# The opening group's two quads take x together: four output banks per k-tile, and the opening loads in one fixed line

## The chip, the cores and the metric

The kernel runs on one core of one Trainium2 chip. The metric is the device time in microseconds (us) of one execution. Three runs of the kernel before took 868.64, 869.21 and 869.86 us (median 869.21). A separate profiled execution gave the trace that is read here.

The engines go by short names: PE is TensorE (matmuls), PEld its weight loads, DVE is VectorE, ACT is ScalarE, POOL is GpSimd, SP is SyncE, which issues nearly all DMA transfers. A name such as SPq or ACTq means the sequencer that issues DMAs.

## The reference

One layer of a hybrid decoder: meta tokens are put ahead of the sequence, the input is normalised, projected by one matrix into eight parts, and goes through a gated short convolution and a chunkwise retention; an output projection, the residual and a last norm follow. What the change touches is the first part of the projection.

```python
h = jnp.concatenate([meta_b, x], axis=1)        # 16 meta rows, then 2048 rows of 1024
hn = rms_norm(h, norm_g)
proj = jnp.einsum('bld,de->ble', hn, w_in)      # w_in: 1024 x 4096
cx, cb, cc, cg, q, k, v, rg = jnp.split(proj, N_PROJ, axis=-1)
conv_out = short_conv_branch(cx, cb, cc, conv_w) * jax.nn.silu(cg)
...
mixed = jnp.concatenate([conv_out, ret_out], axis=-1)
return h + jnp.einsum('ble,ed->bld', mixed, w_out)
```

All of it is in float32. The kernel gets that precision by splitting each operand into a high part and a low part (`mh`, `ml` for x and for the opening's weights, `wh`, `wl` for later weights) and adding three products.

## The kernel before, in words

**Tiles.** The sequence is worked in two blocks of 1024 rows (`r` = 0, 1), each in two column halves `j` of 512. The contraction over 1024 is cut into eight k-tiles of 128, four to a half. A *quad* is one pair of projection parts (2 x 128 output columns) for a block, so four output tiles 128x512, each in one PSUM bank. The pool `pj` has four banks, the pool `ms` four others for everything small.

**Two kinds of quad.** `quad` (L236) forms a quad by seven products of sums of blocks (Strassen's scheme); it needs sums and differences of x-blocks, held in `m[2]`, `m[3]`, `m[4]`, `m[6]`, and of weight blocks. `stationary` makes the weight blocks: POOL forms sums and differences in place (L121, L124, L124, L151), ACT casts the high parts (L112), DVE subtracts to get the low parts (L113). `quad_plain` (L293) forms a quad the ordinary way, 96 matmuls, and needs no sums. The first group of all, a convolution group (`group_plain`), uses it twice, since x is still arriving then: the first quad is `first[0]` (parts CC and CX), the second `first[1]` (CG and CB). Head 0 with its first `quad` comes next.

**The opening.** The x-tiles (256 KB each, eight per column half) are loaded by SP in `load_x`, scaled and split: ACT makes `mh` (L115), DVE `ml` (L116). The weights of the first quad are loaded in two pieces for the two blocks that are needed first (128 columns on ACT's queue, 384 on SP's), the other two whole (`begin`). `moving` runs over j, half and k-tile, and calls hooks after given tiles. `normalise_meta` prepares the meta rows, `meta_products` (L456) multiplies the raw weight blocks with them, and `block_sums` (L189, L192, L124) makes the sums of x-blocks. `row_factors` squares the rows of x (ACT L407, sixteen tiles for a block, eight to a factor) and turns the sums into the norm's factors: `rsqrt_mean` on POOL (L309), `rot` on DVE (L314), a spreading matmul on PE (L340).

**What sets the order.** A scheduler orders the instructions of each engine by priorities and its own estimate of time; each engine then works its queue strictly in that order, and an instruction that waits holds all that stand behind it. `tc.issue_after(x)` puts an instruction behind another in the schedule. Memory slots are reused in rings: `raw` has eight slots, which the opening's weights, the rows of x and head 0's weights go through; the slot of operand number 2 holds the first quad's weights and later `m[2]`, the slot of number 3 the second quad's weights and later `m[3]`.

**Names used later.** *Product 2* is the third of head 0's seven products. It needs `wl` and `wh` of the block difference that POOL's second L124 leaves in `ra`, and `m[2]`. POOL's first L124 overwrites a raw weight block, so it has to wait until PE's L456 for head 0 has read that block.

## Time and profile before

| | us |
|---|---|
| median of three runs | 869.21 |
| lowest and highest | 868.64, 869.86 |
| the profiled execution, its own time | 868.33 |
| its span (first to last instruction) | 866.5 |
| PE busy in the span | 855.4 |
| DVE busy | 725.7 |
| ACT busy | 497.8 |
| POOL busy | 394.6 |

The span is the trace's own clock; 1.83 us of the profiled execution lie around it. Times in the trace count from the start of the span. A busy PE is not yet a PE at its best pace, since matmuls overlap and their ends are modelled; so what PE loses is read from the starts of its matmuls and not from its busy share. The granted clock is at full speed in all forty slices of the page, which is the 2.4 GHz level.

### The profile page before, as it was taken

The numbers are of one execution on the slowest core, as the hardware profiler recorded it, in microseconds if no ns is written. First come the engines' busy times: TensorE is split into PE (matmuls) and PEld (weight loads), VectorE is DVE, ScalarE is ACT, GpSimd is POOL, SyncE is SP. The second block draws the span as 40 slices with busy tenths as digits, with TensorE's granted clock in tenths as the row PEclk, the third lists the DMA queues.
The fourth block names the chain that finished last, engine by engine and source line by source line (L and its number), as shares of the span: only waits on it lengthen the run. The fifth ranks groups of instructions, "written<-read, shape, count | busy, mean of one in ns | idle before, by whom it ended". The sixth has DMA issues, their size and how long they took to land.

```text
span 866.5 us, 12699 instructions
## 1 busy us (share of the span) xinstructions
PE 855.4 (99%) x4216; PEld 705.1 (81%) x4216; DVE 725.7 (84%) x1194; ACT 497.8 (57%) x899; POOL 394.6 (46%) x286
## 2 busy tenths in 40 slices
PE   9999999999999999999999999999999999999996
PEld 6778888888787778788888888888888888788885
DVE  7899988888988977989789898988767799877663
ACT  8676548384755554948374757544333566545553
POOL 0662332423145554352242323354746555677773
PEclk9999999999999999999999999999999999999999
DMA  9724235454656633845264845646123584555431
GB/s 339 233 79 89 72 85 154 113 149 135 159 169 190 199 98 98 313 149 146 62 158 121 159 134 124 205 113 216 48 78 81 173 326 136 169 165 178 156 134 73
DMA packets 127218, 129.51 MB, mean 149 GB/s; under 512 B 58352, under 2 KB 75568, under 8 KB 127152
## 3 DMA queue, kind: packets, MB, share of 16 engines
q1 hardware_dynamic: 126576, 128.30, 50.0%
q8 instruction: 33, 0.54, 0.3%
q10 hardware_dynamic: 576, 0.40, 0.1%
q14 instruction: 33, 0.27, 0.1%
HBM read 90.91 MB, written 25.17 MB: 134 GB/s over the span
## 4 chain that ended last, share of the span: by engine, by line
PE 78%; DVE 6%; issue 1%; ACT 0%; POOL 0%; POOLq 0%; DVEq 0%
PE pj L236 66%; PE pj L293 5%; PE ms L831 1%; PE ms L820 1%; PE ms L830 1%; PE ms L807 1%; DVE wl L113 1%; PE ms L456 1%; DVE ml L113 1%; DVE ml L116 0%; DVE yo L121 0%; DVE yo L906 0%; DVE yo L941 0%; ACT n L407 0%; DVE tc L121 0%
## 5 line engine op out<-in xcount | busy, mean ns | idle before, releaser
L236 PE MATMUL pj<-mh,wl 128*128 128x512 f32 x1008 | 396.0, 393 | 1.3 <-DVE wl L113 0.7
L236 PE MATMUL pj<-mh,wh 128*128 128x512 f32 x1008 | 393.1, 390 | 0.0
L236 PE MATMUL pj<-ml,wh 128*128 128x512 f32 x1008 | 392.9, 390 | 0.0
L112 ACT CAST wh<-ra 128x512 fp32r<-128x512 f32 x216 | 133.9, 620 | 232.1 <-PE pj L236 193.6
L236 PEld LDWEIGHTS pj<-mh,wl 128*128 128x128 f32 x1008 | 189.3, 188 | 43.1 <-issue 1.5
L113 DVE TENSOR_TENSOR wl<-ra,wh 128x512 fp32r<-128x512 f32 x216 | 192.4, 893 | 36.6 <-ACT wh L112 35.2
L236 PEld LDWEIGHTS pj<-mh,wh 128*128 128x128 f32 x1008 | 189.3, 188 | 39.4
L236 PEld LDWEIGHTS pj<-ml,wh 128*128 128x128 f32 x1008 | 189.3, 188 | 38.1
L121 POOL TENSOR_TENSOR sa<-ra 128x512 f32<-128x512 f32 x36 | 54.1, 1504 | 108.8 <-DMA ra<-in_w_in 50.5
L124 POOL TENSOR_TENSOR ra<-sa,ra 128x512 f32<-128x512 f32 x36 | 51.3, 1424 | 81.8 <-DVE wl L113 79.6
L124 POOL TENSOR_TENSOR ra<-ra 128x512 f32<-128x512 f32 x36 | 59.1, 1641 | 59.2 <-PE ms L456 48.9
L151 POOL TENSOR_TENSOR ra<-ra 128x512 f32<-128x512 f32 x36 | 61.5, 1709 | 47.3 <-issue 35.2
L243 ACT COPY tc<-pj 128x512 f32<-128x512 f32 x108 | 62.6, 580 | 0.1
L293 PE MATMUL pj<-mh,mh 128*128 128x512 f32 x128 | 51.0, 401 | 0.6 <-ACT mh L115 0.6
L293 PE MATMUL pj<-mh,ml 128*128 128x512 f32 x128 | 50.0, 390 | 1.0 <-DVE ml L113 1.0
L293 PE MATMUL pj<-ml,mh 128*128 128x512 f32 x128 | 48.0, 391 | 0.0
L843 POOL TENSOR_TENSOR rp<-rs,neg_half 128x4 f32<-128x4 f32 x16 | 19.4, 1211 | 46.4 <-DVE rs L121 46.2
L596 POOL TENSOR_TENSOR c<-c,rr 128x512 f32<-128x512 f32 x14 | 25.7, 1834 | 22.2 <-DVE c L637 14.1
L906 DVE TENSOR_TENSOR yo<-pj,yo 128x512 f32<-128x512 f32 (+1 forms) x33 | 22.0, 671 | 15.9 <-PE pj L236 8.5
L917 POOL TENSOR_TENSOR z<-yo,final_g 128x512 f32<-128x512 f32 x16 | 26.8, 1674 | 18.6 <-DVE yo L906 18.6
L847 DVE TENSOR_SCALAR pm<-ms,mv,rp 128x128 f32<-128x128 f32 x64 | 21.9, 403 | 11.8 <-POOL rp L843 11.8
L112 ACT CAST wh<-sa 128x512 fp32r<-128x512 f32 x36 | 22.2, 618 | 16.0 <-PE pj L236 15.8
(153 smaller groups left out, 1223.2 us busy)
## 6 DMA issues: line engine op xcount, KB each, us to landing
ra<-in_w_in SPq DMA_DIRECT2D x126, 256.0 KB, 2.9
x<-in_xT SPq DMA_DIRECT2D x48, 256.0 KB, 5.0
w<-in_w_out SPq DMA_DIRECT2D x32, 256.0 KB, 4.7
ra<-mixed SPq DMA_DIRECT2D x32, 256.0 KB, 2.7
yo<-in_x SPq DMA_DIRECT2D x32, 256.0 KB, 4.6
ra<-in_x SPq DMA_DIRECT2D x16, 256.0 KB, 3.3
mixed<-c SPq DMA_DIRECT2D x16, 256.0 KB, 2.5
sums_x<-x SPq DMA_DIRECT2D x16, 256.0 KB, 2.8
```

Source lines behind the costliest of these rows:

```text
L112: nc.scalar.copy(out=hi, in_=src)
L113: lowered[0] = eng.tensor_tensor(out=lo, in0=src, in1=hi.bitcast(F32), op=ALU.subtract)
L121: eng.tensor_tensor(out=out, in0=a, in1=b, op=ALU.add)
L124: eng.tensor_tensor(out=out, in0=a, in1=b, op=ALU.subtract)
L151: summed[0] = nc.gpsimd.tensor_tensor(out=a12, in0=a12, in1=a11, op=ALU.subtract)
L236: nc.tensor.matmul(bank, a[:, ks], b, start=first and kt == 0 and n == 0, stop=kt == KH - 1 and n == 2, skip_group_check=not first,)
L243: copied[0] = nc.scalar.copy(out=c, in_=bank)
L293: nc.tensor.matmul(banks[i], a[:, ks], b, start=half + kt + n == 0, stop=half == 1 and kt == KH - 1 and n == 2,)
L596: eng.tensor_tensor(out=out, in0=a, in1=b, op=ALU.mult)
L847: nc.vector.tensor_scalar(out=y[:, cs], in0=o[:, cs], scalar1=mv[:, c, 0:1], scalar2=rp[:, c, :], op0=ALU.subtract, op1=ALU.mult,)
L906: last[0] = nc.vector.tensor_tensor(out=y[:, cs], in0=pp[:, cs], in1=y[:, cs], op=ALU.add)
L917: nc.gpsimd.tensor_tensor(out=ys[i][j], in0=y, in1=final_g[:, j * HB : (j + 1) * HB], op=ALU.mult)
```

## The change

The two quads of the opening group no longer run one after the other. A new function, `quads_plain`, goes through x once per column half and gives every k-tile to both quads, so that a k-tile has twelve matmuls instead of six and four banks are open at once. All opening loads on SP go through `in_line`, which ties each to the one before it in the schedule. The weights of both quads are loaded early, in pieces (`split_pieces`), and x-tiles stand behind them by name (`behind`). Everything that is not needed for the first products (sums, rows, tables, the meta rows) is put behind the last load of the line.

```diff
-        nc.scalar.mul(hi, src, scale)
+        scaled[0] = nc.scalar.mul(hi, src, scale)
...
+    def quads_plain(ws, m, takes):
+        for j in range(2):
+            banks = [[ps_proj() for _ in range(2)] for _ in ws]
+            for half in range(2):
+                for kt in range(KH):
+                    ks = slice(kt * P, (kt + 1) * P)
+                    mh, ml = m[BLOCK[half][j]][kt]
+                    for n, w in enumerate(ws):
+                        for i in range(2):
+                            wh, wl = w[2 * i + half]
+                            for s, (a, b) in enumerate(((wh, mh), (wl, mh), (wh, ml))):
+                                nc.tensor.matmul(
+                                    banks[n][i], a[:, ks], b, start=half + kt + s == 0,
+                                    stop=half == 1 and kt == KH - 1 and s == 2,
+                                )
+            for n, take in enumerate(takes):
+                for i in range(2):
+                    take(i, j, banks[n][i], None)
...
+    def in_line(out, src):
+        with tc.issue_after(line[0].ins) if line[0] else nullcontext():
+            line[0] = nc.sync.dma_start(out, src)
...
-        quad_plain(first[0], m, take)
-        meta_carry(g, meta)
...
-        quad_plain(first[1], m, take)
+        quads_plain(first, m, (take_inner, take_outer))
+        meta_carry(g, meta)
...
-    opening = {n: raw() for n in (0, 2)}
-    for n, a in opening.items():
-        nc.scalar.dma_start(a[:, PIECES[0]], t["w_in"][2 * NG, n][:, PIECES[0]])
+    opening = {(q, n): raw() for q in range(2) for n in (0, 2)}
...
+    for n in (0, 2):
+        nc.scalar.dma_start(opening[0, n][:, PIECES[0]], t["w_in"][2 * NG, n][:, PIECES[0]])
...
+            after = {
+                (0, 0): lambda: (begin(0), split_pieces(0)),
+                (0, 1): lambda: split_pieces(1),
+                (0, KH - 1): lambda: begin(1),
+                (0, KT - 1): lambda: (pieces.append(scaled[0]), meta_behind()),
+            }
...
-            first.append(plain_parts(w_loads(2 * NG + 1)))
-            load_tables()
...
+            with tc.issue_after(line[0].ins):
+                load_tables()
...
+                    with tc.issue_after(pieces[2].ins):
+                        block_sums(b11, b12, b22, b21, t1[kt], t3[kt], gain_of(kt), gain_of(KH + kt), nc.gpsimd)
```

How the built program moves on the engines is shown at three places. Numbers behind a name tell one tile from another; they differ between the two programs.

PE at its first k-tile, before. Of the two names behind the arrow the first is the x-tile, the second the weight block:

```order
L293 MATMUL pj<-mh_123,mh_127 128x512
L293 MATMUL pj<-mh_123,mh_130 128x512
L293 MATMUL pj<-mh_123,ml_128 128x512
L293 MATMUL pj<-ml_124,mh_127 128x512
L293 MATMUL pj<-mh_123,ml_131 128x512
L293 MATMUL pj<-ml_124,mh_130 128x512
L293 MATMUL pj<-mh_143,mh_127 128x512
```

PE at the same place, after:

```order
L318 MATMUL pj<-mh_125,mh_131 128x512
L318 MATMUL pj<-mh_125,mh_135 128x512
L318 MATMUL pj<-mh_125,mh_139 128x512
L318 MATMUL pj<-mh_125,mh_143 128x512
L318 MATMUL pj<-mh_125,ml_132 128x512
L318 MATMUL pj<-ml_126,mh_131 128x512
L318 MATMUL pj<-mh_125,ml_140 128x512
L318 MATMUL pj<-ml_126,mh_139 128x512
L318 MATMUL pj<-mh_125,ml_136 128x512
L318 MATMUL pj<-ml_126,mh_135 128x512
L318 MATMUL pj<-mh_125,ml_144 128x512
L318 MATMUL pj<-ml_126,mh_143 128x512
```

The first x-tile now meets four weight blocks in twelve matmuls, where it met two in six before the second x-tile (`mh_143`) was wanted.

PE at the end of the opening group, before: L340 spreads the second norm factor, L494 and L456 are the meta rows' work, L236 is head 0's first product.

```order
L340 MATMUL ms<-rot,ones 128x512
L494 MATMUL ms<-ident,mk 128x16
L456 MATMUL ms<-ra,meta_s 16x128 x16
L293 MATMUL pj<-mh_256,mh_302 128x512
...
L293 MATMUL pj<-ml_263,mh_308 128x512
L236 MATMUL pj<-mh_123,wl 128x512
```

PE at the same place, after (L364, L527, L489 and L239 are the same four lines):

```order
L318 MATMUL pj<-mh_292,ml_198 128x512
L318 MATMUL pj<-ml_293,mh_197 128x512
L364 MATMUL ms<-rot,ones 128x512
L527 MATMUL ms<-ident,mk 128x16
L489 MATMUL ms<-ra,meta_s 16x128 x16
L239 MATMUL pj<-mh_125,wl 128x512
```

Twelve matmuls of the opening stood between the meta rows' products and head 0; now none does.

DVE at the same time, before: the first `wl<-ra` in the list is the low part that product 2 needs.

```order
L113 TENSOR_TENSOR ml_690<-t_318,mh_689 128x512
L495 COPY carry_79<-ms 128x2
L534 TENSOR_TENSOR u<-u,rr_373 128x512
L534 TENSOR_TENSOR cb<-cb,rr 128x512
L113 TENSOR_TENSOR ml_686<-t_317,mh_685 128x512
L113 TENSOR_TENSOR wl<-ra,wh 128x512
L113 TENSOR_TENSOR ml_694<-t_319,mh_693 128x512
```

DVE at the same place, after:

```order
L113 TENSOR_TENSOR ml_345<-x,mh_344 128x512
L567 TENSOR_TENSOR u<-pj,u 128x512
L113 TENSOR_TENSOR ml_371<-x,mh_370 128x512
L113 TENSOR_TENSOR ml_692<-t_323,mh_691 128x512
L528 COPY carry_79<-ms 128x2
L113 TENSOR_TENSOR ml_700<-t_325,mh_699 128x512
L567 TENSOR_TENSOR cb<-cb,rr 128x512
L567 TENSOR_TENSOR u<-u,rr_379 128x512
L113 TENSOR_TENSOR wl<-ra,wh 128x512
```

Three full-size operations have moved ahead of that `wl`: the low part of one block of `m[2]` (`ml_345`), the product out of the second bank of `pj`, and `ml_700`, which stood behind it as `ml_694`. POOL's queue has the same order in both programs, and behind product 2's low part the queues of the other engines have too.

## Rows read from the trace of the kernel before

**Rows 1.** The page, part 1: busy time, share and instructions by engine.

```profile
PE 855.4 (99%) x4216; PEld 705.1 (81%) x4216; DVE 725.7 (84%) x1194; ACT 497.8 (57%) x899; POOL 394.6 (46%) x286
```

**Rows 2.** Timeline of PE in the opening: start, length (us), line, tiles, idle before.

```profile
4.87 1.31 PE L293 MATMUL pj<-mh,mh 128*128 128x512 f32 x2
...
6.72 0.40 PE L293 MATMUL pj<-ml,mh 128*128 128x512 f32 x1
7.75 0.50 PE L293 MATMUL pj<-mh,mh 128*128 128x512 f32 x1 [0.64 <-ACT mh L115]
8.09 0.40 PE L293 MATMUL pj<-mh,ml 128*128 128x512 f32 x1
```

**Rows 3.** Timeline of ACT in the same stretch.

```profile
3.84 0.72 ACT L115 ACTIVATE mh<-x,gain 128x512 fp32r<-128x512 f32 x1 [0.20 <-DMA gain<-in_norm_g]
4.48 0.30 ACT L1008 CAST mh<-ra 128x128 fp32r<-128x128 f32 x1
5.33 1.13 ACT L1008 CAST mh<-ra 128x128 fp32r<-128x128 f32 x3 [0.55 <-DMA ra<-in_w_in]
6.37 0.72 ACT L192 ACTIVATE x<-x,gain 128x512 f32<-128x512 f32 x1
6.99 1.94 ACT L115 ACTIVATE mh<-x,gain 128x512 fp32r<-128x512 f32 x3
```

**Rows 4.** DMAs issued between 2.13 and 2.5 us: size, us from issue to landing.

```profile
x<-in_xT SPq DMA_DIRECT2D x1, 256.0 KB, 4.0
```

**Rows 5.** DMAs issued between 1.7 and 1.9 us.

```profile
ra<-in_w_in ACTq DMA_DIRECT2D x1, 64.0 KB, 3.7
```

**Rows 6.** One window: busy of PE, PEld, DVE, ACT, POOL; clock, DMA share, GB/s.

```profile
5.00:10.00 5.00, 4.37 (x18) 2.88 (x17) 4.13 (x9) 4.67 (x10) 0.00 (x0) 1.00 0.99 356
```

**Rows 7.** Timeline of PE from the meta products to head 0's product 2.

```profile
51.85 1.07 PE L456 MATMUL ms<-ra,meta_s 128*16 128x128 f32 x32
...
55.71 0.39 PE L236 MATMUL pj<-mh,wl 128*128 128x512 f32 x1
...
61.15 0.39 PE L236 MATMUL pj<-mh,wl 128*128 128x512 f32 x1
```

**Rows 8.** Timeline of DVE from the first norm factor to product 2's low part.

```profile
29.43 1.78 DVE L113 TENSOR_TENSOR ml<-x,mh 128x512 fp32r<-128x512 f32 x1 [1.18 <-ACT mh L112]
...
35.07 0.16 DVE L121 TENSOR_TENSOR ss<-ss 128x4 f32<-128x4 f32 x1 [2.05 <-ACT ra L407]
...
48.99 0.69 DVE L314 TENSOR_TENSOR rot<-ident,rc 128x512 f32<-128x512 f32 x1 [0.32 <-POOL rc L309]
...
51.56 3.10 DVE L113 TENSOR_TENSOR ml<-t,mh 128x512 fp32r<-128x512 f32 x5
54.58 0.15 DVE L495 COPY carry<-ms 128x2 f32<-128x2 f32 x1
54.64 1.71 DVE L534 TENSOR_TENSOR u<-u,rr 128x512 f32<-128x512 f32 x1
...
59.69 0.68 DVE L113 TENSOR_TENSOR wl<-ra,wh 128x512 fp32r<-128x512 f32 x1
```

**Rows 9.** DVE's busy time from 35 to 60 us, the sum of five windows.

```profile
sum 25.00, DVE 23.33; mean DVE 4.67
```

**Rows 10.** Timeline of POOL: a pair of x-block sums, then head 0's weight blocks.

```profile
23.00 7.67 POOL L124 TENSOR_TENSOR t<-x 128x512 f32<-128x512 f32 x2 [6.38 <-DVE x L189]
...
53.05 2.75 POOL L124 TENSOR_TENSOR ra<-ra 128x512 f32<-128x512 f32 x1 [4.10 <-DVE ml L113]
55.88 1.62 POOL L124 TENSOR_TENSOR ra<-sa,ra 128x512 f32<-128x512 f32 x1
57.59 1.63 POOL L151 TENSOR_TENSOR ra<-ra 128x512 f32<-128x512 f32 x1
```

**Rows 11.** Timeline of ACT: the high part that product 2 needs.

```profile
57.54 0.62 ACT L112 CAST wh<-ra 128x512 fp32r<-128x512 f32 x1 [1.21 <-POOL ra L124]
```

**Rows 12.** SP's own waits up to 60 us: us in total, times, longest.

```profile
SPq L367 <- DVE ml L113: 5.0, 3, 3.9
```

More of the change, by code (lines that the diff above doesn't have):

```diff
@@ L165, in parts, with moving @@
         m[i].append((hi, lo))
-    def moving(load, scale=None, after={}):
+    scaled = [None]
+    def moving(load, scale=None, after={}, behind={}):
         m = [[] for _ in range(8)]
@@ L176, in moving @@
                     blocks.append(load(k, j))
-                    parts(m, BLOCK[half][j], kt, blocks[-1], scale(k) if scale else None)
+                    with tc.issue_after(behind[j, k]().ins) if (j, k) in behind else nullcontext():
+                        parts(m, BLOCK[half][j], kt, blocks[-1], scale(k) if scale else None)
                     after.get((j, k), lambda: None)()
@@ L988, in hybrid_trunk @@
         if r == 0:
[L989 to L990 removed]
+            w = [[None] * 4 for _ in range(2)]
             def begin(half):
                 if half:
[L994 to L995 removed]
+                    for q, slot in enumerate((FIRST_W, PLAIN_W)):
+                        for n in (1, 3):
+                            w[q][n] = plain_part(n, lambda a: in_line(a, t["w_in"][2 * NG + q, n]), slot)
@@ L996, in begin @@
                     return
-                for n, a in opening.items():
-                    w[n] = a, operand(FIRST_W, n)
-                    nc.sync.dma_start(a[:, PIECES[1]], t["w_in"][2 * NG, n][:, PIECES[1]])
-                done = []
-                for cs in PIECES:
-                    with ExitStack() as behind:
-                        for ins in done:
-                            behind.enter_context(tc.issue_after(ins.ins))
-                        for n, a in opening.items():
-                            hi, lo = w[n][1]
-                            done = [
-                                nc.scalar.copy(out=hi[:, cs], in_=a[:, cs]),
-                                nc.vector.tensor_tensor(
-                                    out=lo[:, cs], in0=a[:, cs], in1=hi[:, cs].bitcast(F32), op=ALU.subtract
-                                ),
-                            ]
@@ L1032, in hybrid_trunk, with split_pieces @@
-            nc.sync.dma_start(conv_w, t["conv_w"])
-            nc.sync.dma_start(ret_g, t["ret_norm_g"])
+                for n in (0, 2):
+                    fetch(1, n, PIECES[0])
+            def split_pieces(at):
+                cs = PIECES[at]
+                if at:
+                    for q, n in opening:
+                        fetch(q, n, cs)
+                with tc.issue_after(scaled[0].ins):
+                    for (q, n), a in opening.items():
+                        if at == 0:
+                            w[q][n] = a, operand((FIRST_W, PLAIN_W)[q], n)
+                        hi, lo = w[q][n][1]
+                        cast = nc.scalar.copy(out=hi[:, cs], in_=a[:, cs])
+                        nc.vector.tensor_tensor(
+                            out=lo[:, cs], in0=a[:, cs], in1=hi[:, cs].bitcast(F32), op=ALU.subtract
+                        )
+                pieces.append(cast)
@@ new lines, in hybrid_trunk, with meta_behind @@
+            pieces = []
+            def meta_behind():
+                with tc.issue_after(line[0].ins):
+                    normalise_meta()
+            after = {
[4 more added lines that the diff above has]
+            }
+            m, b = moving(load_x(r), gain_of, after, {(0, k): lambda k=k: pieces[k > 1] for k in range(1, KH)})
@@ new lines, in hybrid_trunk @@
+            first = [[p for a, p in tiles] for tiles in w]
+            blocks = None, meta_products([a for a, p in w[0]])
+            with tc.issue_after(line[0].ins):
+                load_tables()
+                nc.sync.dma_start(cols, t["cols"])
+                t3 = [a[:, i * HB : (i + 1) * HB] for a in (row_tile("t3", 1) for _ in range(2)) for i in range(2)]
+                t1 = [brief("t1") if n < BRIEF else sb.tile([P, HB], F32, name="t1", tag="tc", bufs=COPIES) for n in range(KH)]
+                for kt in range(KH):
+                    b11, b21, b12, b22 = (b[n * KH + kt] for n in range(4))
+                    with tc.issue_after(pieces[2].ins):
+                        block_sums(b11, b12, b22, b21, t1[kt], t3[kt], gain_of(kt), gain_of(KH + kt), nc.gpsimd)
+                    parts(m, 2, kt, b22)
+                    parts(m, 6, kt, b21)
+                for _ in row_factors(0, f):
+                    pass
+                nc.sync.dma_start(causal, t["causal"])
+                nc.sync.dma_start(conv_w, t["conv_w"])
+                nc.sync.dma_start(ret_g, t["ret_norm_g"])
```

35 lines of the change are left out of this document (11 added, 24 removed).

## The prediction

> **What bounds the kernel now.** I read the page first: PE is busy 855.4 us of a span of 866.5 us, 99% [rows 1]. So a change pays only where it closes a hole between PE's matmuls, and costs only where it opens one. Holes are read from PE's timeline, by the distance between starts. The undisturbed distance comes from head 0: 24 matmuls lie between 55.71 and 61.15 [rows 7], 5.44 / 24 = 0.2267 us each.
>
> In the opening, six matmuls of the first k-tile start from 4.87 on, and the seventh, the first of the second k-tile, at 7.75 [rows 2]. That is 2.88 us where six need 1.36: 1.52 us lost. The next distance, 8.09 - 7.75 = 0.34, is 0.11 too long as well. The hole is 1.63 us in all, and from there to head 0 nothing comparable stands in PE's timeline. What made it stands on ACT: the casts of weight pieces wait 0.55 us for a DMA until 5.33, then ACT scales an x-tile for the block sums at 6.37 (L192, 0.72 us), and only at 6.99 makes the second x-tile's high part, which PE waited for [rows 2, 3]. The second x-tile itself had landed at 2.12 + 4.0 = 6.1 [rows 4].
>
> The other end of the opening is head 0, and there DVE decides. From 35 to 60 us it is busy 23.33 of 25.00 us [rows 9]. Its last piece of work that PE needs at once, the low part for product 2, runs from 59.69 to 60.37 [rows 8], and product 2 starts at 61.15 [rows 7]: 0.78 us to spare.
>
> **The change part by part.** Everything between the first matmul and product 2 is the same work for PE, so I ask one question: when does product 2 of head 0 start, against 61.15? Two chains lead there, and the later one sets it.
>
> *Chain one, PE's own.* The first matmul stays where it is, at 4.87: it needs the first x-tile (ACT at 3.84) and the first piece (ACT at 4.48), both in the same places of ACT's queue as before [rows 3]. A k-tile now has twelve matmuls, 2.72 us. The second matmul wants the second piece on ACT's queue. That one landed 3.7 us after its issue at 1.66, at about 5.3, while SP's 192 KB pieces were under way beside it [rows 5]; SP's first pieces are now 64 KB. If all four are there when ACT comes, the four casts follow each other and PE loses about 0.1 us; if the second is as late as now, 5.3 + 0.3 for the cast + 0.2 until PE sees it - 5.1 = 0.7. I take 0.3, nearer the lower end, since fewer bytes stand beside it. The first k-tile then ends at 4.87 + 2.72 + 0.3 = 7.9. The second x-tile has 256 KB of pieces ahead of it instead of 512, so it lands no later than 6.1, and ACT, whose L192 has gone behind the x-tiles, needs 0.72: ready at 6.9, a microsecond early. After that supply is ahead: half of a column half takes PE 48 x 0.2267 = 10.9 us, and by its end 3.1 MB must have come, 8.8 us at 356 GB/s [rows 6]. So the hole shrinks from 1.63 to 0.3 us; chain one puts head 0 at 55.71 - 1.3 = 54.4 and product 2 at 54.4 + 5.44 = 59.8. The bounds are a gain of 0.9 and of 1.5.
>
> Four banks at once leave none for the next column half, so its first matmul waits for a copy of the first bank. That bank's last matmul stands nine before the end, 2.0 us, and a copy takes 0.6; twenty matmuls into that one bank, 4.5 us, then cover the other three. I price it at nothing. At head 0 the same bank has, besides nine matmuls, the norm's spreading matmul and the meta products in between, 4 us. The four loads of the second quad go past x in SP's queue; PE has them 10 us ahead of need. `normalise_meta` goes behind the line; its result is first needed by the meta products at about 36 us, and is ready near 32.
>
> *Chain two, DVE's.* Between the operation that opens the first norm factor (`ss`, 35.07) and product 2's low part, DVE now has three full operations more, as the order shows: the slots of `m[2]` are held by the first quad's weights, which are in use until the opening's end. One takes (3.10 - 0.68) / 4 = 0.605 us [rows 8]; three take +1.8 us. Two things pull the other way. The first row tiles were held up on SP by DVE's opening low parts, 3.9 us at the longest [rows 12]; those are done early now, so the eighth square and with it `ss` come sooner. The ring of four free slots then sets their pace, and ACT's copies of three banks go between, so I give it 0.7 us, with 0 and 1.3 as ends. And of DVE's 25.00 - 23.33 = 1.67 us of idle time [rows 9] up to half may be filled: 0 to 0.8, 0.4 taken. POOL's operations that shut DVE out cost the same number of turns in both (below). Low part done: 60.37 + 1.8 - 0.7 - 0.4 = 61.1; product 2 about 0.1 later, at 61.2, with 60.1 and 62.3 as ends.
>
> *Sum.* Chain two is the later: 61.2 against 61.15, +0.05 us; the gain of 1.3 us is handed back as a wait at product 2. The profiled execution would go from 868.33 to 868.4. The median of three stood 0.88 above it, so the forecast on that scale is 869.3.
>
> **A rule weighed.** At 54.64 DVE's operation takes 1.71 us instead of 0.68, and two more like it follow, one to each of POOL's three operations from 53.05 to 59.2 [rows 8, 10]: about 1.1 us of shutting out each. But POOL's pair from 23.00 on took 7.67 us, until DVE paused for 1.18 us before 29.43 [rows 8, 10]; there DVE operations that started later went first. The Trainium skill, SBUF — State Buffer, section "Who interferes with whom", says that a VectorE instruction with two SBUF inputs and a GpSimd one that reads SBUF exclude each other, and that whichever starts first holds the port for its whole length. By it POOL would always get its turn at DVE's next boundary and rival B below would be out; the trace agrees at 54.64 and not at 23.00.
>
> **The rivals.**
>
> A. *DVE keeps up.* If `ss` comes early and idle time fills, low part and POOL are done before PE is, and chain one counts: product 2 at 59.8, -1.3 us, 867.9. For it: from POOL's first subtraction to the low part's end an undisturbed run takes two operations of about 1.45, a cast from its start of 0.6 and 0.68, 4.2 us in all, and PE leaves 5.2. Against it: DVE's queue is full.
>
> B. *POOL starts too late (slower).* POOL's first subtraction waits for the meta products. These ended 2.8 us before head 0 began: POOL started at 53.05, PE reached product 2 at 61.15, 8.1 us later [rows 7, 10]. Now nothing stands between them and head 0; POOL starts 0.2 us after head 0 does, at 54.6, and PE wants the result 5.2 us later. The chain took 60.37 - 53.05 = 7.3 us before, which gives 61.9; if POOL's first has to wait for a pause of DVE, as at 23.00, until about 57, it is 57 + 1.1 + 0.6 + 1.1 + 0.7 (cast, with what lies before it [rows 11]) + 1.8 (a shut-out low part) = 62.3, and one more turn of 1.7 makes 64.0. So +1.2 to +2.9, middle +1.9: 871.2. It decides from where POOL's second subtraction ends after 59.7, that is when the pair takes more than 5.1 us; from 53.05 it took 4.45.
>
> C. *The change does not do what it says.* A piece or tile comes late in the new line, PE loses as much at 5 to 8 us as before or more, and chain two is as long: about +0.9 us, 870.2.
>
> **How the numbers follow.** Forecast 0.52, at 869.3, with its own range 868.2 to 870.4 from chain two's ends; A 0.22, B 0.20, C 0.06. To hold 8 in 10 the range takes in most of A (867.9, less the 0.2 that chain one may give beyond 1.3) and the lower part of B: 867.7 to 870.9. About 0.2%, 1.74 us, is what a measurement of this kernel tells from no change. Faster by that means below 867.47: more than the whole hole of 1.63 us is worth, so 0.05, for a stall elsewhere that goes too. Slower means above 870.95: a good half of B, 0.12. The rest, 0.83, is no change that can be told.
>
> **What would show it.** Right: PE's seventh matmul follows without a hole and the second k-tile begins near 7.9; head 0 begins near 54.4; then PE waits about 1.4 us at product 2 for DVE's `wl` (L113). A: no wait there, and the whole program 1.3 us ahead. B: the wait is over 2.5 us and ACT's cast before it waits for POOL's L124. C: PE waits for ACT or a DMA between 5 and 10 us. Wrong altogether: a wait for the four banks near 28 us, or a difference that arises behind head 0, where the queues have the same order.

## The result: slower by 0.2%

The changed kernel takes 871.05 us (median of 14 runs, 869.46 to 873.47) against 869.52 for the kernel before (median of 14 runs beside it, 868.64 to 871.68). The ratio is 1.0020, with a 95% interval of 1.0010 to 1.0029. The forecast was 869.3 with a range of 867.7 to 870.9: no measurable change was forecast, and the result is 0.15 us above the range, on the slow side. The profiled execution went from 868.33 to 870.28 us, +1.95.

The page, part 1, of the kernel after, against [rows 1]: busy time, share and instructions by engine.

```profile
PE 856.1 (99%) x4216; PEld 705.5 (81%) x4216; DVE 725.3 (84%) x1196; ACT 498.9 (57%) x901; POOL 387.9 (45%) x286
```

PE runs the same 4216 instructions, and its busy time grows by only 0.7 us while the span grows by 2.0; the rest is idle time. Two places make the difference.

**The opening.** PE's timeline of the kernel after, against [rows 2]: start, length (us), line, tiles, idle before.

```profile
4.87 0.99 PE L318 MATMUL pj<-mh,mh 128*128 128x512 f32 x1
6.07 1.37 PE L318 MATMUL pj<-mh,mh 128*128 128x512 f32 x3 [0.21 <-ACT mh L1046]
...
9.11 0.62 PE L318 MATMUL pj<-mh,mh 128*128 128x512 f32 x2
```

ACT's timeline of the same stretch, against [rows 3].

```profile
4.34 0.48 ACT L1046 CAST mh<-ra 128x128 fp32r<-128x128 f32 x2
5.72 0.50 ACT L1046 CAST mh<-ra 128x128 fp32r<-128x128 f32 x2 [0.90 <-DMA ra<-in_w_in]
6.24 0.72 ACT L115 ACTIVATE mh<-x,gain 128x512 fp32r<-128x512 f32 x1
```

The first matmul stands at 4.87 as before, the second at 6.07 instead of 5.10. The second k-tile begins at 9.11, 4.24 us after the first matmul, where twelve matmuls need 2.72: a hole of 1.52 us, against 1.63 before. The hole has not shrunk; it has moved from the second x-tile to the first weight pieces.

**Product 2 of head 0.** PE's, DVE's, POOL's and ACT's timelines of the kernel after, in that order, against [rows 7, 8, 10, 11].

```profile
60.76 0.39 PE L239 MATMUL pj<-mh,wh 128*128 128x512 f32 x1
62.81 0.47 PE L239 MATMUL pj<-mh,wl 128*128 128x512 f32 x1 [1.66 <-DVE wl L113]
```

```profile
35.23 0.16 DVE L121 TENSOR_TENSOR ss<-ss 128x4 f32<-128x4 f32 x1 [0.62 <-ACT ra L431]
...
56.09 1.37 DVE L113 TENSOR_TENSOR ml<-x,mh 128x512 fp32r<-128x512 f32 x1
57.38 1.78 DVE L113 TENSOR_TENSOR ml<-t,mh 128x512 fp32r<-128x512 f32 x1
59.08 0.15 DVE L528 COPY carry<-ms 128x2 f32<-128x2 f32 x1
59.15 1.71 DVE L113 TENSOR_TENSOR ml<-t,mh 128x512 fp32r<-128x512 f32 x1
60.78 0.68 DVE L567 TENSOR_TENSOR cb<-cb,rr 128x512 f32<-128x512 f32 x1
61.39 0.68 DVE L567 TENSOR_TENSOR u<-u,rr 128x512 f32<-128x512 f32 x1
61.99 0.68 DVE L113 TENSOR_TENSOR wl<-ra,wh 128x512 fp32r<-128x512 f32 x1
```

```profile
55.62 1.29 POOL L124 TENSOR_TENSOR ra<-ra 128x512 f32<-128x512 f32 x1 [4.82 <-ACT rr L365]
56.98 1.62 POOL L124 TENSOR_TENSOR ra<-sa,ra 128x512 f32<-128x512 f32 x1
```

```profile
58.64 0.62 ACT L112 CAST wh<-ra 128x512 fp32r<-128x512 f32 x1 [1.64 <-POOL ra L124]
```

PE was done with products 0 and 1 by 60.99 (60.76 + 0.23) and stood idle until 62.81: 1.82 us, released by DVE's low part. The operand of that low part had been ready on ACT at 59.26. From there it waited for its place in DVE's queue until 61.99, behind three operations that PE did not need yet. Product 2 starts 1.66 us later than before (61.15); the remaining 0.29 us of the 1.95 arose behind it.

### The profile page after: what moved, and what is told of

Its sections match the earlier page's. It is cut to its first block, busy times and chain, and to the rows that moved or that the text cites. A ratio compares the mean times of both kernels' runs of the same rounds, so it can differ in the third digit from the quotient of the medians.

```text
span 868.5 us, 12704 instructions
## 1 busy us (share of the span) xinstructions
PE 856.1 (99%) x4216; PEld 705.5 (81%) x4216; DVE 725.3 (84%) x1196; ACT 498.9 (57%) x901; POOL 387.9 (45%) x286
## 4 chain that ended last, share of the span: by engine, by line
PE 77%; DVE 6%; issue 2%; ACT 0%; POOL 0%; POOLq 0%; DVEq 0%
PE pj L239 66%; PE pj L296 5%; PE ms L863 1%; PE ms L852 1%; PE ms L862 1%; PE ms L839 1%; DVE wl L113 1%; PE ms L489 1%; DVE ml L113 1%; DVE yo L121 0%; DVE ml L116 0%; DVE yo L938 0%; DVE yo L973 0%; ACT n L431 0%; DVE tc L121 0%
## 5 line engine op out<-in xcount | busy, mean ns | idle before, releaser
L239 PE MATMUL pj<-mh,wl 128*128 128x512 f32 x1008 | 396.4, 393 | 3.4 <-DVE wl L113 2.8
L239 PE MATMUL pj<-mh,wh 128*128 128x512 f32 x1008 | 393.1, 390 | 0.0
L239 PE MATMUL pj<-ml,wh 128*128 128x512 f32 x1008 | 392.9, 390 | 0.0
L239 PEld LDWEIGHTS pj<-mh,wl 128*128 128x128 f32 x1008 | 189.3, 188 | 45.9 <-ACT wh L112 3.4
L239 PEld LDWEIGHTS pj<-mh,wh 128*128 128x128 f32 x1008 | 189.2, 188 | 39.7
L239 PEld LDWEIGHTS pj<-ml,wh 128*128 128x128 f32 x1008 | 189.3, 188 | 37.9
L949 POOL TENSOR_TENSOR z<-yo,final_g 128x512 f32<-128x512 f32 x16 | 26.8, 1677 | 18.6 <-DVE yo L938 18.6
L627 POOL TENSOR_TENSOR c<-c,tc 128x512 f32<-128x512 f32 x14 | 24.0, 1714 | 18.3 <-ACT tc L653 18.1
L121 DVE TENSOR_TENSOR tc<-pj,tc 128x512 f32<-128x512 f32 x28 | 19.2, 685 | 14.4 <-PE pj L239 13.3
L113 DVE TENSOR_TENSOR ml<-t,mh 128x512 fp32r<-128x512 f32 x32 | 28.9, 935 | 1.6 <-ACT mh L112 1.6
```

The costliest lines, as they stand in the source:

```text
L113: lowered[0] = eng.tensor_tensor(out=lo, in0=src, in1=hi.bitcast(F32), op=ALU.subtract)
L121: eng.tensor_tensor(out=out, in0=a, in1=b, op=ALU.add)
L239: nc.tensor.matmul(bank, a[:, ks], b, start=first and kt == 0 and n == 0, stop=kt == KH - 1 and n == 2, skip_group_check=not first,)
L627: eng.tensor_tensor(out=out, in0=a, in1=b, op=ALU.mult)
L949: nc.gpsimd.tensor_tensor(out=ys[i][j], in0=y, in1=final_g[:, j * HB : (j + 1) * HB], op=ALU.mult)
```

## The experiments

Two theories stood against each other from here. The **DVE theory**: product 2 waits for the low part's place in DVE's queue, which holds three operations more than before. The **POOL theory** (rival B): the chain over POOL's subtractions begins too late, since the meta products now stand directly before head 0. A third, the **opening theory**, says that the total follows the opening's holes. The ratio in the table is to the kernel before, run beside it on the same chip (its median lay between 869.1 and 869.5), with a 95% interval; it is not the quotient of the two medians. The last three columns are read from the profiled execution of each kernel (where head 0's first matmul and product 2 start, and how long PE waits there).

| kernel | median us | ratio (95%) | head 0 | product 2 | PE's wait there |
|---|---|---|---|---|---|
| before | 869.1 to 869.5 | 1 | 55.71 | 61.15 | 0 |
| after | 871.05 | 1.0020 (1.0010 to 1.0029) | 55.41 | 62.81 | 1.82 |
| dve | 869.01 | 0.9998 (0.9990 to 1.0007) | 55.17 | 60.78 | 0.03 |
| meta_pure | 870.19 | 1.0011 (1.0002 to 1.0021) | 57.28 | 62.90 | 0 |
| pairs | 870.12 | 1.0009 (1.0000 to 1.0017) | 55.14 | 62.49 | 1.78 |
| dve_pairs | 869.27 | 1.0001 (0.9992 to 1.0009) | 54.95 | 60.62 | 0.08 |
| nosums | 870.57 | 1.0012 (1.0004 to 1.0021) | 54.86 | 62.26 | 1.82 |
| half | 869.04 | 0.9994 (0.9985 to 1.0003) | 55.19 | 61.38 | 0.61 |
| whole | 869.54 | 1.0001 (0.9992 to 1.0009) | 54.85 | 60.45 | 0.02 |
| whole6 | 869.38 | 1.0004 (0.9995 to 1.0012) | 54.98 | 60.56 | 0 |
| before_act | 870.17 | 1.0013 (1.0003 to 1.0023) | 55.83 | 63.08 | 1.81 |
| half_gp | 870.59 | 1.0017 (1.0008 to 1.0026) | 56.48 | 62.63 | 0.58 |
| half_gp_whole | 871.98 | 1.0032 (1.0021 to 1.0043) | 56.70 | 62.53 | 0.25 |

### dve: work that PE does not need yet, behind the low part

```diff
-        w += [parts(a) for a in (a11, s1, a21)]
+        w.append(parts(a11))
+        third[0] = lowered[0]
+        w += [parts(a) for a in (s1, a21)]
...
-            for j in range(2):
-                mul(nc.vector, u[j][:, 2:], u[j][:, 2:], rr2[j])
+            with tc.issue_after(third[0].ins):
+                for j in range(2):
+                    mul(nc.vector, u[j][:, 2:], u[j][:, 2:], rr2[j])
...
-                mul(nc.vector, gate, gate, rr[j])
+                with tc.issue_after(third[0].ins):
+                    mul(nc.vector, gate, gate, rr[j])
```

> The four products of `complete` (u and gate by the norm factors) stand behind product 2's low part on DVE; all else as in the changed kernel. There the low part starts at 61.99 us, 2.8 us after ACT has its high part ready (59.2), and PE waits 1.8 us for it. DVE theory (the low part's place in DVE's queue sets product 2): four operations of 0.6 us fewer stand ahead of it, the low part starts between 59.6 and 60.2, PE's wait falls from 1.8 to 0.0 to 0.3 us, the whole run is 1.5 to 1.8 us below the changed kernel: the level of the kernel before, within 0.5 us. POOL theory (its subtractions begin too late): the chain over POOL and ACT is untouched, product 2 stays within 0.4 us of 62.8, the total of the changed kernel stays.

Timelines of the kernel dve: POOL, ACT, DVE and then PE.

```profile
55.37 1.64 POOL L124 TENSOR_TENSOR ra<-ra 128x512 f32<-128x512 f32 x1 [5.48 <-PE ms L491]
57.09 1.62 POOL L124 TENSOR_TENSOR ra<-sa,ra 128x512 f32<-128x512 f32 x1
```

```profile
58.74 0.62 ACT L112 CAST wh<-ra 128x512 fp32r<-128x512 f32 x1 [1.83 <-POOL ra L124]
```

```profile
56.00 1.56 DVE L113 TENSOR_TENSOR ml<-t,mh 128x512 fp32r<-128x512 f32 x1
59.39 1.24 DVE L113 TENSOR_TENSOR wl<-ra,wh 128x512 fp32r<-128x512 f32 x1 [1.83 <-ACT wh L112]
```

```profile
60.52 0.39 PE L241 MATMUL pj<-mh,wh 128*128 128x512 f32 x1
60.78 0.47 PE L241 MATMUL pj<-mh,wl 128*128 128x512 f32 x1
...
80.79 0.47 PE L241 MATMUL pj<-mh,wl 128*128 128x512 f32 x1 [0.39 <-ACT pl L712]
```

The low part now starts at 59.39, as soon as ACT's high part is there, and DVE stands idle for 1.83 us ahead of it. PE goes from product 1 to product 2 with 0.26 us between starts, so the wait is gone. The median falls by 2.0 us, back to the level of the kernel before. The POOL theory is out as the cause of the 1.8 us: POOL's second subtraction ends at 58.71 (58.60 in the kernel after) and ACT's high part starts at 58.74 (58.64), and yet the time is back. But that chain is the next limit: it starts 0.2 us after head 0 does, and product 2 starts only 0.03 us after PE could have taken it. The price is a new hole of 0.55 us at 80.79, where none stood in the kernel after.

### meta_pure: POOL's chain earlier, DVE's queue as it is

```diff
+        with ExitStack() as behind:
+            while lows:
+                behind.enter_context(tc.issue_after(lows.pop().ins))
+            w.append(parts(a11))
...
+                    end = (j, half, kt) == (1, 1, KH - 1)
+                    if end:
+                        near()
+                    with tc.issue_after(product[0].ins) if end else nullcontext():
...
                         parts(m, i, kt, held[kt])
+                    lows.append(lowered[0])
```

(`near` loads head 0's blocks and traces its meta products; product 2's low part is held behind every instruction in `lows`.)

> Head 0's meta products go ahead of the opening's last twelve matmuls, as in the kernel before, so POOL's subtractions begin some 2.6 us earlier; the same operations stay ahead of product 2's low part on DVE. DVE theory: the low part ends within 0.6 us of 62.7, PE still waits 1.2 to 1.9 us, total within 0.6 us of the changed kernel. POOL theory: product 2 starts 1.5 to 1.8 us earlier, the wait is gone and the total is that of the kernel before.

POOL, DVE and PE of the kernel meta_pure.

```profile
55.78 1.30 POOL L124 TENSOR_TENSOR ra<-sa,ra 128x512 f32<-128x512 f32 x1
```

```profile
51.37 0.68 DVE L348 TENSOR_TENSOR rot<-ident,rc 128x512 f32<-128x512 f32 x1
...
61.73 0.68 DVE L113 TENSOR_TENSOR wl<-ra,wh 128x512 fp32r<-128x512 f32 x1
```

```profile
52.11 1.12 PE L374 MATMUL ms<-rot,ones 128*128 128x512 f32 x2 [1.73 <-DVE rot L348]
```

POOL's second subtraction ends at 57.08, 1.5 us sooner than in the kernel after (58.60), and the low part still starts at 61.73. That much is as the DVE theory has it. What neither theory foresaw is where PE waits: not at product 2 but 1.9 us at 52.11, for `rot`, the diagonal of the second norm factor. Its spreading matmul had to go ahead of the meta products, so with them it came twelve matmuls forward, and DVE, in the same full queue, makes `rot` only at 51.37. DVE's lateness reached PE through another operand. With the wait at another place the run says less about the total than was hoped.

### pairs and dve_pairs: the opening's first k-tile in ACT's order

```diff
-                    for n, w in enumerate(ws):
-                        for i in range(2):
...
-                            for s, (a, b) in enumerate(((wh, mh), (wl, mh), (wh, ml))):
...
+                    for i in range(2):
+                        with tc.issue_after(last.ins) if opened and last else nullcontext():
+                            for s in range(3):
+                                for n, w in enumerate(ws):
```

(`opened` is true in the first k-tile alone; `last` is the last matmul of the first pair of blocks.)

> The opening's first k-tile alone is ordered anew on PE: the six matmuls of the two blocks that ACT casts first, then the six of the other two. In the changed kernel the second matmul wants a block that ACT casts third; holes of 0.98, 0.36 and 0.16 us follow. Expected in either theory: these holes shrink to 0.3 us together and head 0 begins near 54.2 instead of 55.4. DVE theory: product 2 still starts at 62.8 within 0.4, PE's wait there grows from 1.8 to some 3.0 us, total within 0.4 us of the changed kernel. Opening theory (the total follows the opening's holes): 1.2 us below the changed kernel.

PE of the kernel pairs.

```profile
5.00 1.28 PE L322 MATMUL pj<-mh,mh 128*128 128x512 f32 x2
6.08 0.74 PE L322 MATMUL pj<-ml,mh 128*128 128x512 f32 x2
...
62.49 0.47 PE L239 MATMUL pj<-mh,wl 128*128 128x512 f32 x1 [1.62 <-DVE wl L113]
```

Half of the opening's hole is closed (0.75 us instead of 1.50), but the first matmul stood 0.13 later in this run, and head 0 begins only 0.27 us earlier. The wait at product 2 stays at 1.78. The expected 54.2 for head 0 was missed by 0.9. Product 2 and the wait are as the DVE theory has them; the median is 0.9 us below the kernel after, more than the 0.4 expected, though the two intervals overlap. By its total the run lies nearer to the opening theory's 1.2 us, so the times alone do not separate the two here.

> Both edits at once: the first k-tile by pairs on PE, and the four products behind product 2's low part on DVE. DVE theory: head 0 near 54.2, product 2 between 59.6 and 60.4, the total 2.3 to 3.0 us below the changed kernel and 0.8 to 1.4 us below the kernel before, though neither edit alone gets below the kernel before. Opening theory: 1.2 us below the changed kernel. POOL theory: no faster than the changed kernel.

PE of the kernel dve_pairs.

```profile
9.50 0.50 PE L324 MATMUL pj<-mh,mh 128*128 128x512 f32 x1 [0.32 <-ACT mh L1054]
...
60.62 0.47 PE L241 MATMUL pj<-mh,wl 128*128 128x512 f32 x1
```

With both edits the first k-tile has a hole of 0.27 us, but the second then runs out of weights at 9.50 for 0.48 us. Head 0 gains 0.22 us on dve, and the time is that of dve (1.0001). The expected 0.8 to 1.4 us below the kernel before did not come: once PE takes its first tiles faster, the loads are what it waits for.

### whole, whole_only, whole6: what the line of loads can bring

One window of the kernel before, of the kernel after and of dve_pairs: busy time of PE, PEld, DVE, ACT, POOL; granted clock, DMA share, GB/s.

```profile
4.00:5.00 1.00, 1.00 (x5) 0.41 (x3) 0.41 (x1) 0.78 (x2) 0.00 (x0) 1.00 1.08 335
```

```profile
4.00:5.00 1.00, 1.00 (x5) 0.45 (x3) 0.53 (x1) 0.82 (x3) 0.00 (x0) 1.00 0.46 113
```

```profile
4.00:5.00 1.00, 1.00 (x5) 0.36 (x3) 0.33 (x1) 1.00 (x3) 0.00 (x0) 1.00 0.47 50
```

From 4 to 5 us the DMA engines moved 335 GB/s before, and 113 and 50 with the new line (59, 68 and 74 in dve, pairs and meta_pure). The kernel whole loads the second quad's first two blocks in one piece:

```diff
-                    fetch(1, n, PIECES[0])
+                    fetch(1, n, slice(0, HB))
...
-                    for q, n in opening:
-                        fetch(q, n, cs)
+                    for n in (0, 2):
+                        fetch(0, n, cs)
```

> As dve_pairs, and the second quad's two first blocks come whole (256 KB each) where they came as a 64 KB piece and later a 192 KB piece: two transfers fewer in the opening line, and none of 64 KB on SP. In the five runs so far with 64 KB pieces on SP the DMA engines moved 50 to 113 GB/s from 4 to 5 us, where the kernel before moved 335. Line theory (SP issues one transfer in 0.47 us, and 64 KB each leave the engines idle): over 250 GB/s from 4 to 5 us, the third x-tile lands near 8.2 instead of 10.4, the holes from 5 to 11 us fall from 0.97 to under 0.5 us, head 0 starts near 54.4. With product 2's low part early on DVE this goes through: 0.4 to 0.8 us below dve_pairs. Rival (the stall is one of the memory, whatever the size): the same 50 to 113 GB/s and no gain.

The same window of the kernel whole.

```profile
4.00:5.00 1.00, 1.00 (x5) 0.45 (x3) 0.47 (x1) 0.94 (x3) 0.00 (x0) 1.00 1.03 345
```

The rate is back at 345 GB/s, and at 312 and 340 in the two profiles below; the third x-tile lands at 8.76 instead of 10.43. So it is the 64 KB pieces on SP that leave the engines idle. At the start SP issues one transfer every 0.47 us, of 64, 192 or 256 KB alike, so pieces of 64 KB cannot bring more than about 139 GB/s (65,536 bytes in 0.47 us); why the rate lies even below that is not shown. But the gain in time did not come. Head 0 starts at 54.85, 0.10 before dve_pairs, and the median is 0.3 above it, with overlapping intervals. The holes from 5 to 11 us add up to 0.88 us, where under 0.5 was expected (0.97 in dve_pairs). The longest, 0.56 us, stands before the second matmul, and the trace names nothing that PE waited for there.

> The profile of the same kernel as whole a second time: how far its opening repeats. Expected: rate from 4 to 5 us and head 0 within 15% and 0.3 us of whole's.

A second profile of the same kernel (869.92 us, one run) shows how far such an opening repeats: the rate is there again (312 GB/s), but the second quad's second block lands at 6.75 instead of 6.34, ACT's second piece at 6.93 instead of 5.07, PE loses 0.74 us waiting for the casts of these two, and head 0 starts at 55.29. The 0.3 us that were expected as its spread are exceeded. Tenths of a microsecond in the opening are therefore not to be read from one profile.

```diff
-FIRST_W, PLAIN_W, B12 = 2, 3, 4
+FIRST_W, PLAIN_W, B12 = 6, 3, 4
```

> As whole, and the first quad's weights stand in slot 6 instead of slot 2: then the operands of product 2 can be made before the opening ends, and those of product 6 must wait. DVE theory: the full operations between the first norm factor and product 2's low part stay as many (26 or 27), since those of product 6 take their places in the queue, so product 2 moves by less than 0.4 us; total within 0.4 us of whole. Rival (the slots were the cause by a wait of product 2's own operands): 0.5 us or more below whole.

DVE of the kernel whole6.

```profile
59.11 1.23 DVE L113 TENSOR_TENSOR wl<-ra,wh 128x512 fp32r<-128x512 f32 x1 [3.21 <-ACT wh L112]
```

The numbers are those that the DVE theory expected: product 2 at 60.56 against 60.45, the median 0.2 us lower, and 24 operations of full size between the first norm factor and the low part in both kernels (26 or 27 were expected). But the run does not test the slots. In whole PE no longer waited at product 2 (0.02 us), and here the low part waits for ACT, with DVE idle for 3.21 us ahead of it; so the rival had nothing to win. Whether other slots would help the changed kernel itself stays untested.

### before_act and nosums: one part of the change alone, and the change without it

```diff
# before_act, on the kernel before
-                block_sums(b11, b12, b22, b21, t1[kt], t3[kt], gain_of(kt), gain_of(KH + kt), nc.gpsimd)
+                with tc.issue_after(behind_x[0].ins):
+                    block_sums(b11, b12, b22, b21, t1[kt], t3[kt], gain_of(kt), gain_of(KH + kt), nc.gpsimd)
# nosums, on the kernel after
-                    with tc.issue_after(pieces[2].ins):
+                    if True:
                         block_sums(b11, b12, b22, b21, t1[kt], t3[kt], gain_of(kt), gain_of(KH + kt), nc.gpsimd)
```

> The kernel before with one part of the change alone: ACT scales the x-tiles for the block sums only behind the eighth x-tile, so the second x-tile's high part starts 0.6 us earlier. Expected on PE: the hole of 0.81 us at 7.75 falls to 0.2, head 0 starts at 55.1. DVE theory: product 2's low part had 0.78 us of slack; DVE gets the scaling for the sums later, so part of the 0.6 us is lost as a wait there: total 0 to 0.5 us below the kernel before. Opening theory: the full 0.6 us.

DVE and then PE of the kernel before_act.

```profile
36.72 0.16 DVE L121 TENSOR_TENSOR ss<-ss 128x4 f32<-128x4 f32 x1 [3.45 <-ACT ra L407]
...
62.25 0.68 DVE L113 TENSOR_TENSOR wl<-ra,wh 128x512 fp32r<-128x512 f32 x1
```

```profile
63.08 0.47 PE L236 MATMUL pj<-mh,wl 128*128 128x512 f32 x1 [1.65 <-DVE wl L113]
```

This one went to the other side: 1.0013, slower. Head 0 did not gain (55.83 instead of the expected 55.1): the second weight piece on ACT's queue landed at 6.05 instead of 5.31, and PE lost 1.33 us before its second matmul. ACT took the scaling off the second x-tile's way, and `ss`, which waits for ACT's squares, comes at 36.72 instead of 35.07; that the postponed work made the squares late is argued here, not shown. DVE's queue shifts with it, the low part starts at 62.25 instead of 59.69, and PE waits 1.81 us at product 2. The distance from `ss` to the low part grew too, by 0.9 us, with the same operations in between. So the wait of the changed kernel appears here without its four banks, its line of loads and its three operations more.

> The changed kernel without one of its parts: ACT's scaling of x-tiles for the block sums is no longer held behind the eighth x-tile and stands between the first casts again, two of its operations of 0.72 us ahead of the piece casts and the third x-tile. DVE's order up to product 2 stays nearly the same. DVE theory: the opening's holes grow by 0.7 to 1.4 us and head 0 starts that much later, PE's wait at product 2 shrinks from 1.8 by the same amount, total within 0.4 us of the changed kernel. Opening theory: 0.7 to 1.4 us above the changed kernel.

PE of the kernel nosums.

```profile
5.93 0.96 PE L318 MATMUL pj<-mh,mh 128*128 128x512 f32 x3 [0.64 <-ACT mh L1046]
...
62.26 0.47 PE L239 MATMUL pj<-mh,wl 128*128 128x512 f32 x1 [1.66 <-DVE wl L113]
```

The opening did not get longer, as was expected, but shorter: its hole is 1.0 us and head 0 starts at 54.86. ACT's scaling seems to stand in time in which ACT waits for weights anyway (0.23 and 0.54 us of such waits stood from 8 to 10 us in the kernel after). PE's wait at product 2 is 1.82 us, as in the kernel after. The low part moved up by the same 0.55 us as head 0; the total is 0.5 us below the kernel after (0.4 expected), with intervals that overlap. The opening theory had the sign the other way only through the wrong guess about the hole; this run speaks neither for it nor against it.

### half, half_gp, half_gp_whole: is there a version that beats both?

In half only the second column half's two products stand behind the low part. Against dve:

```diff
-                with tc.issue_after(third[0].ins):
+                with tc.issue_after(third[0].ins) if j else nullcontext():
                     mul(nc.vector, gate, gate, rr[j])
```

(The two products of u are treated alike.)

> As dve, but of the four products of `complete` only the two of the second column half stand behind product 2's low part; the other two keep their places near 51 us. In dve DVE stood idle for 1.8 us before that low part, and a new hole of 0.55 us came at 80.8 in head 0's second quad, where the work moved back was still being caught up. DVE theory: the two fill the idle time, product 2 still starts as soon as PE is free (a wait under 0.3 us), and the hole at 80.8 falls to 0.1 or nothing: total 0 to 0.5 us below dve. Rival (any one operation more ahead of the low part costs its 0.6 us): a wait of 0.6 to 1.2 us at product 2, total 0.3 to 0.9 us above dve.

PE of the kernel half.

```profile
61.38 0.47 PE L241 MATMUL pj<-mh,wl 128*128 128x512 f32 x1 [0.45 <-DVE wl L113]
```

The hole at 80.8 is gone, and 0.61 us stand at product 2 instead. That is the rival of its expectation for the wait and the DVE theory for the other hole: each operation more ahead of the low part costs something there. The median is 869.04 against 869.16 for the kernel before, ratio 0.9994 with an interval that holds 1. It is the lowest ratio of all, and no kernel here is shown to be faster than the kernel before.

```diff
-    nc.scalar.dma_start(gain, t["norm1_g"])
+    nc.gpsimd.dma_start(gain, t["norm1_g"])
```

> half and pairs together, and the gain column is loaded over POOL's queue, so that ACT's queue issues its two weight pieces 0.45 us earlier. Expected: ACT's second piece lands near 5.3 instead of 5.7, the hole before the first k-tile's second pair falls under 0.2 us, head 0 starts at 54.4 to 54.8 instead of 55.0, and the total is 0.2 to 0.6 us below half. If POOL's queue brings the gain later than 3.9 us, the first matmul is late by as much and the gain is lost.

PE and ACT of the kernel half_gp.

```profile
5.65 0.74 PE L324 MATMUL pj<-mh,mh 128*128 128x512 f32 x2 [0.25 <-ACT mh L1054]
...
54.26 1.12 PE L370 MATMUL ms<-rot,ones 128*128 128x512 f32 x2 [0.99 <-DVE rot L344]
```

```profile
60.27 0.62 ACT L112 CAST wh<-ra 128x512 fp32r<-128x512 f32 x1 [2.56 <-POOL ra L124]
```

The last sentence of the expectation came true: POOL's queue issued the gain at 1.24, it landed at 4.67, and the first matmul stands at 5.65. PE waits for DVE's `rot` as well, as in meta_pure, and the ratio is 1.0017, where 0.2 to 0.6 us below half was expected. The 0.58 us at product 2 have another cause than in the kernel after: the low part starts at 60.92, as soon as ACT's high part is done (60.89), and that waited for POOL. Here POOL's chain is the limit.

> As half_gp, with the second quad's first two blocks loaded whole. Expected: 310 GB/s or more from 4 to 5 us, the third x-tile lands by 9, holes from 5 to 11 us together under 0.6 us, head 0 at 54.3 to 54.7; total at or up to 0.4 us below half_gp, the lowest of all kernels here: 0.8 to 1.5 us below the kernel before.

The gain landed at 5.07 there, the first matmul stands at 6.05, and the time is the longest of all (1.0032), where the lowest was expected. POOL's chain sets product 2 here too (a wait of 0.25 us). The profiled execution, 869.97 us, is the shortest of the twelve of this kernel (up to 874.34), so what made the others so long is not in this trace.

## Why the prediction was wrong, point by point

**The place was right, the size was not.** The prediction asked when product 2 of head 0 starts, named DVE's queue as the chain that sets it, and expected PE to wait there for `wl`. All three are in the trace. The start was given as 61.2, with 62.3 as the upper end; it was 62.81.

**The step that failed: chain two's credits.** The sum for the low part's end was 60.37 + 1.8 - 0.7 - 0.4 = 61.1; measured 62.67. The +1.8 for three operations was right in kind. The two credits did not exist. The first, 0.7 us for an earlier `ss`, came out as a loss of 0.16 (35.23 against 35.07). The prediction argued from [rows 12] that SP had been held up by DVE's low parts. That hold-up is gone: SP issues the first row tile at 18.48 instead of 23.48. But the tile lands only at 26.57 (26.16 before), and ACT, which squares it, then still waits for PE's first bank, with the squares behind that copy in its queue. ACT of the kernel after, and a window that begins with the same copy (columns as in [rows 6]):

```profile
27.02 0.59 ACT L572 COPY u<-pj 128x512 f32<-128x512 f32 x1 [2.71 <-PE pj L318]
```

```profile
27.02:35.20 8.18, 8.18 (x37) 6.51 (x36) 6.53 (x10) 8.18 (x23) 1.67 (x1) 1.00 0.56 176
```

From 27.02 to 35.20 ACT is busy for 8.18 of 8.18 us. SP in turn waits for ACT: up to 60 us, in total, times, longest:

```profile
SPq L391 <- ACT ra L431: 7.5, 10, 1.5
SPq L1082 <- DMA rot_t<-in_rot: 3.7, 1, 3.7
```

The first line is the ring of row tiles, whose slots ACT's squares free. The wait of 3.7 us for `rot_t` ends at 25.85, before the first square, and the next row tile is issued only behind that square, at 28.26; so it is not what held `ss`.

The second credit, 0.4 us of idle time to be filled, has the wrong sign too. Windows from `ss` to the start of the low part, before and after, then the end of the second one:

```profile
35.07:59.69 24.62, 24.62 (x139) 19.29 (x132) 23.01 (x40) 19.94 (x49) 16.38 (x9) 1.00 0.43 150
```

```profile
35.23:61.99 26.76, 25.92 (x165) 19.81 (x163) 24.70 (x43) 21.17 (x50) 15.44 (x10) 1.00 0.40 135
44.42:61.99 17.57, 16.73 (x99) 12.85 (x97) 17.57 (x26) 13.79 (x28) 11.15 (x9) 1.00 0.17 63
```

DVE's idle time is 2.06 us instead of 1.61, 0.45 more. All of it lies before 44.42, where DVE waits for ACT (1.58 us before 37.39, 0.41 before 44.42); from there to the low part DVE has none. The three added operations run at 54.89, 55.49 and 59.15, so the idle time lay ahead of them and could not take them up. With the measured values in place of the credits the sum gives 60.37 + 1.8 + 0.16 + 0.45 = 62.78, 0.1 from the 62.67 measured. Even the upper end of 62.3, which takes both credits at nothing, was too early, since both came out as losses.

How far the count of operations sets the place shows across the runs. The count is that of 128x512 operations between `ss` and the low part in DVE's built order.

| kernel | operations | `ss` | low part starts | distance |
|---|---|---|---|---|
| before | 25 | 35.07 | 59.69 | 24.6 |
| before_act | 25 | 36.72 | 62.25 | 25.5 |
| half | 26 | 35.26 | 60.56 | 25.3 |
| nosums | 28 | 34.92 | 61.44 | 26.5 |
| pairs | 28 | 34.96 | 61.67 | 26.7 |
| after | 28 | 35.23 | 61.99 | 26.8 |
| meta_pure | 28 | 34.97 | 61.73 | 26.8 |

With 24 operations (dve, dve_pairs, whole, whole6), and in half_gp and half_gp_whole, the low part no longer waits for its place but for ACT. Three operations more cost 1.9 to 2.2 us against the kernel before, but 1.0 to 1.3 against before_act, which has the same 25: the count sets the place to within about a microsecond, and the waits for ACT do the rest.

**Chain one: a gain of 1.3 us was expected, 0.3 came** (head 0 at 55.41 instead of 55.71, forecast 54.4). The bounds for the second matmul's wait were 0.1 and 0.7 us; it was 0.98, and 0.36 and 0.16 more followed. Two errors made it. ACT cast the first pieces of both quads first, PE's second matmul is of the first quad's second piece, and the two orders were not laid beside each other; pairs showed that this is worth half of the hole. And the argument that fewer bytes beside it would bring the second piece sooner is not borne out: it landed at 5.70 instead of 5.31, at 5.41 to 5.87 in the seven kernels with 64 KB pieces on SP that issue it at the same time, and at 5.07 to 6.93 in the five profiles with larger ones. But this error did not set the time, since product 2 waited for DVE.

**Priced rightly at nothing:** the four banks. No PE hole over 0.11 us stands near the middle of the opening; nor did the line's delays to `normalise_meta` open one.

**Rival A** is out: DVE did not keep up. **Rival B** gave 871.2 and the result is 871.05, yet its mechanism is not what happened: POOL's two subtractions took 2.98 us (55.62 to 58.60) where it needed more than 5.1, and dve took the whole wait away with POOL's chain as it was. It is a right time for a wrong reason, and luck. Its chain does come next, once the low part stands early in DVE's queue (half_gp). **Rival C** described the opening nearly as it came (a piece late in the new line, the hole as long as before), with a chance of 0.06, and expected 870.2. It came together with the DVE wait, and the forecast had treated them as alternatives.

**The rule weighed** on the port that POOL and DVE share: at 56.09, 57.38 and 59.15 three DVE operations took 1.37, 1.78 and 1.71 us beside POOL's three, as three did before [rows 8], and DVE's wait for its turn is part of the queue's lateness. POOL's pair was not kept waiting here; the long wait of 23.00 in [rows 10] did not come back at this place. At this place the trace agrees with the Trainium skill, SBUF — State Buffer, section "Who interferes with whom", by which whichever of the two starts first holds the port and the other waits.

**What stays open:** the 0.29 us behind product 2. Matched one by one in PE's order, the matmuls start 1.87 us later than before at 270 us and 2.28 later at 301, and 0.1 of that is given back by the end; what did it is not shown. Open is also the spread of the changed kernel's times: 4.0 us from lowest to highest, 3.0 in the kernel before beside it, 2.4 in dve. Three of its four executions over 872 us have the lowest mean granted clock of the fourteen (0.995, 0.995, 0.996); where in them the clock fell, no trace shows.

## What to carry to other kernels

When a hole at one place is to be closed, look first at the next operand that is just in time, and at where its engine's idle time lies: here DVE had 2 us of it, all before the added operations could run. A credit for "it will start sooner" must name what lets it, and follow that engine's queue too: SP was free earlier, ACT was not. In a queue in program order the ready operand can stand behind work that nobody needs yet; moving four such operations behind it was worth 2.0 us, more than the opening's whole hole of 1.63. And before small pieces are cut for an early start, divide their size by the queue's time for one issue: they cannot bring a higher rate than that.

## What the runs showed of the hardware

- Rate of small transfers: SP issued one transfer in about 0.47 us at the start of the program (at 1.19, 1.66, 2.13 and 2.60 us in the kernel after), so 64 KB pieces offer at most some 139 GB/s on that queue (an estimate: 65,536 bytes / 0.47 us). From 4 to 5 us, all queues together, the engines moved 50 to 156 GB/s with them in eight kernels, and 312 to 385 with 256 KB in their place in four profiles; with the old line it was 335 (before) and 261 (before_act).
- A place in the queue: of two kernels that differ in it alone, the one whose ready operand stood behind four operations more kept PE waiting 1.82 us for it, the other 0.03 (after and dve).
- The same 4 KB load of the gain landed at 3.4 to 4.0 us over ACT's queue (issued at 0.74) and at 4.67 and 5.07 over POOL's (issued at 1.24 and 1.25).
- A 64 KB piece issued at 1.65 to 1.67 us landed anywhere from 5.07 to 6.93 us, in two profiles of one and the same kernel.
